# A decoder layer in split float32 on one core: the mixers' weights split once and reread, value differences in place of a masked subtraction, 512-column queries, early norm sums, and Down's sums on VectorE

## Chip, cores and metric

One core of a Trainium2 chip runs the whole program. The metric is the device time of one execution in microseconds (us), as a median of several runs. The engines are named as the profile names them: PE (TensorE matmuls), PEld (its weight loads), DVE (VectorE), ACT (ScalarE), POOL (GpSimd) and SP (SyncE, which issues most DMAs).

## What is computed

```python
h = rms_norm(x, attn_norm_g);  z = h @ w_in        # 2048 x 1024 by 1024 x 2304
q, k, v, gate_b, gate_c, xc = columns of z          # 8 query heads, 2 key/value heads of 64
q, k = rms_norm(q), rms_norm(k)
y_attn = softmax over 128 keys back, with a learned sink per head     # sliding window
y_conv = gate_b * short_conv(gate_c * xc, conv_w)   # 3 taps, causal
x = x + concat(rms_norm(y_attn), rms_norm(y_conv)) @ w_out
x = x + square(relu(rms_norm(x) @ w_up)) @ w_down   # 1024 -> 4096 -> 1024
```

All inputs and the output are float32; there is one layer and one batch of 2048 positions.

## The kernel before

**Split products.** Each float32 operand of a product is kept as two parts, high and low: the high part is a rounded copy, made by ACT, and the low part is what is left, made by DVE. `mm3` then issues three matmuls (high by high, high by low, low by high), lines L217 to L219.

**Mixers.** The positions go in four chunks of 512 (`CH`), each of four tiles of 128. Per chunk, `project_qkv` computes queries, keys and values in three pieces of 256 columns; `conv_pair` runs twice over the three convolution gates; `out_projection` runs for the convolution half (`part` 1) and, in the next chunk, for the attention half (`part` 0). Each of the 13 weight blocks of a chunk (2048 float32 per partition, 1 MB) is loaded by `load` into one of two `raw` buffers and split by `split` into one of two `whl` buffers: four ACT copies (L193, or L197 with a gain) and four DVE subtractions (L195, L198). The next chunk loads and splits them again.

**Order of the work.** Attention runs block by block (`scores`, then `values`), and between its steps `fill` lets the PE take a number of steps from a generator with the rest of the chunk's matmuls. The numbers are in the table `FILL`; `PRIO` moves groups of instructions earlier or later in the order of ACT, DVE, POOL and SP. Each engine, SP's queue included, works strictly in its own order.

**Attention's second half.** A block of queries sees two blocks of keys with a triangular mask. In `values`, `probabilities` transposes the probabilities into PSUM, makes the high part on ACT (L477) and the low part on DVE (L478); POOL copies out the triangle of the block's own keys (L482, `part`), and DVE subtracts it from the whole (L491), so that `full` holds only the previous block's keys. Then four matmuls (L511) multiply the two with the previous and the own values.

**MLP.** Up and Down are products of 2x2 blocks that are done with seven products in place of eight, so sums of blocks are needed. Down's products come in the order 5, 3, 1, 2, 6, 7, 4; each has 16 groups, and its weights and operands are loaded two steps ahead by `ready_down`, in SP's order. After product 6, `down_out` makes four sums of 128 x 2048 (L819, `tt`, on POOL) for each of two row halves, and stores a finished block with SP (L1183).

Of the kernel before, what the change touches and what calls it, by code (L numbers as in the profile page):

```python
# [7 lines left out]
F32 = mybir.dt.float32  # L8
# [82 lines left out]
def hymba_layer(  # L91
# [50 lines left out]


# [19 lines left out]
    nc.scalar.activation(warm, mhalf[:, :1], AF.Square)  # L163
    mean = const.tile([P, 1], F32, name="mean")
# [14 lines left out]
    def load(src_list, name):  # L179

        raw = pool.tile([P, 2048], F32, tag="raw", name=f"raw_{name}", bufs=2)
        for dst, src in src_list(raw):
            nc.sync.dma_start(dst, src)
        return raw

    def split(raw, name, gains=(None,) * 4, sub=(nc.vector,)):

        hl = pool.tile([P, 2, 2048], F32R, tag="whl", name=f"w_{name}", bufs=2)
        with ahead(7):
            for i, g in enumerate(gains):  # L190
                r = slice(i * 512, (i + 1) * 512)
                if g is None:
                    nc.scalar.copy(hl[:, 0, r], raw[:, r])  # L193
                    eng = sub[i % len(sub)]
                    eng.tensor_tensor(hl[:, 1, r], raw[:, r], hl[:, 0, r].bitcast(F32), op=ALU.subtract)  # L195
                else:
                    nc.scalar.activation(hl[:, 0, r], raw[:, r], AF.Copy, scale=g)  # L197
                    nc.vector.scalar_tensor_tensor(  # L198
                        hl[:, 1, r], raw[:, r], g, hl[:, 0, r].bitcast(F32), op0=ALU.mult, op1=ALU.subtract
                    )  # L200
        return hl

    def weights(src_list, name, **kw_):
        return split(load(src_list, name), name, **kw_)
# [16 lines left out]
    def norm_stats(xt, name):  # L221
# [3 lines left out]
        rs = small.tile([P, 1], F32, tag="rs", name=f"rs_{name}", bufs=2)  # L225
# [87 lines left out]
    z0 = [row("z", f"z0_{t}", NT) for t in range(NT)]  # L313
    raw0 = pool.tile([P, 2048], F32, tag="raw", name="raw_qkv0_0", bufs=2)
    hl0 = pool.tile([P, 2, 2048], F32R, tag="whl", name="w_qkv0_0", bufs=2)
# [3 lines left out]
    def split0(i, eng):  # L319
        r = slice(i * 512, (i + 1) * 512)  # L320
        nc.scalar.copy(hl0[:, 0, r], raw0[:, r])
        eng.tensor_tensor(hl0[:, 1, r], raw0[:, r], hl0[:, 0, r].bitcast(F32), op=ALU.subtract)
# [33 lines left out]
    with tc.tile_pool(name="mix_small", bufs=1) as mix_small, tc.tile_pool(name="mix", bufs=1) as mix:  # L356
# [4 lines left out]
        vz = mix.tile([P, 2, KVH, 2, 2, DH], F32R, name="vz")  # L361
        def project_qkv(c, h, z):

            z += z0 if not c else [row("z", f"z{c}_{t}", NT) for t in range(NT)]
            for pc in range(3):
                hl = hl0 if c + pc == 0 else weights(cols256(wi, pc * 256), f"qkv{c}_{pc}")
                w4 = hl.rearrange("p s (k c) -> p s k c", k=KD)
                for t in range(NT):
                    ps = bank("mm", f"pz{c}_{pc}_{t}")[:, :256]
                    hk = lambda s, k, t=t: h[s][:, k, t * P : (t + 1) * P]  # L370
                    for i in range(3 if c + pc + t == 0 else 0):
                        for k in range(KD):
                            nc.tensor.matmul(
                                ps, hk(i // 2, k), w4[:, i % 2, k, :], start=i + k == 0, stop=i + k == KD + 1
                            )
                    for k in range(KD if c + pc + t else 0):
                        mm3(ps, lambda s, k=k: hk(s, k), lambda s, k=k: w4[:, s, k, :], k == 0, k == KD - 1)
                        if k % 2 and k < KD - 1:
                            yield
                    nc.scalar.copy(z[t][:, pc * 256 : (pc + 1) * 256], ps)  # L380
# [82 lines left out]
        def values(b, zt, sc, n_fill, fill):  # L463
# [3 lines left out]
            def probabilities(kv):  # L467
# [10 lines left out]
                nc.vector.tensor_tensor(p0[:, 1, :], pt, p0[:, 0, :].bitcast(F32), op=ALU.subtract)  # L478
                if b:
                    for i in range(2):  # L480
# [10 lines left out]
                        nc.vector.tensor_tensor(full, full.bitcast(F32), part.bitcast(F32), op=ALU.subtract)  # L491
                    return [(1 - own, pp[0]), (own, pp[1])]
                return [(own, pp[0])]

            with ahead(4):
                for kv in range(KVH):
                    zv = zt[:, O_V + kv * DH : O_V + (kv + 1) * DH]
                    vh = vz[:, own, kv, :, kv, :]
                    nc.scalar.copy(vh, zv[:, None, :].to_broadcast([P, 2, DH]))
# [771 lines left out]
```

## Time and profile before

| what | value |
|---|---|
| time, median of 3 runs | 1991.6 us (1987.71 to 1996.96) |
| the profiled execution | 1995.26 us, with a span of 1993.6 us |
| PE busy | 1949.1 us, 98% of the span |
| DVE, ACT, POOL busy | 66%, 46%, 18% |
| mean granted PE clock | 0.988 of full |

The span runs from the first to the last instruction; the profiled execution's time is 1.7 us more. A matmul is pipelined, so the busy time of PE also covers the tail of each one, and the time from one matmul's start to the next says more of its pace. The stages lie in the span as follows: the first chunk's projection and mixers up to about 168 us, chunks 1 to 3 up to 749, Up to 1372, Down to 1990.

### The profile page before, as it was taken

The numbers are of one execution on the slowest core, as the hardware profiler recorded it, in microseconds if no ns is written. First come the engines' busy times: TensorE is split into PE (matmuls) and PEld (weight loads), VectorE is DVE, ScalarE is ACT, GpSimd is POOL, SyncE is SP. The second block draws the span as 40 slices with busy tenths as digits, with TensorE's granted clock in tenths as the row PEclk, the third lists the DMA queues.
The fourth block names the chain that finished last, engine by engine and source line by source line (L and its number), as shares of the span: only waits on it lengthen the run. The fifth ranks groups of instructions, "written<-read, shape, count | busy, mean of one in ns | idle before, by whom it ended". The sixth has DMA issues, their size and how long they took to land. (4 is left out here: it accounts for less than half of the span.)

```text
span 1993.6 us, 25599 instructions
## 1 busy us (share of the span) xinstructions
PE 1949.1 (98%) x9356; PEld 1630.0 (82%) x9356; DVE 1313.0 (66%) x1964; ACT 919.4 (46%) x1718; POOL 353.7 (18%) x455
## 2 busy tenths in 40 slices
PE   8999999999999999999999999999999999999989
PEld 7879887987988777888888888888888888888877
DVE  4787778678777878877778767666633334545551
ACT  4555455445546546555456555454432232222230
POOL 2231223304132420232201111111000000008000
PEclk9999999999999899999999999999999999999999
DMA  7214522352442379667666454437954447865651
GB/s 244 79 60 116 169 85 84 106 169 64 128 144 100 81 223 314 221 202 224 213 224 231 159 168 137 155 122 260 378 206 148 146 154 239 304 202 179 218 173 43
DMA packets 234190, 342.56 MB, mean 172 GB/s; under 512 B 17232, under 2 KB 148304, under 8 KB 234064
## 3 DMA queue, kind: packets, MB, share of 16 engines
q1 hardware_dynamic: 207120, 271.70, 42.5%
q0 software_dynamic: 13120, 44.05, 6.1%
q10 hardware_dynamic: 13824, 25.17, 3.4%
q8 instruction: 74, 1.21, 0.2%
q14 instruction: 52, 0.43, 0.1%
HBM read 242.31 MB, written 98.57 MB: 171 GB/s over the span
## 5 line engine op out<-in xcount | busy, mean ns | idle before, releaser
L1141 PE MATMUL u<-op_x,wop 128*128 128x512 f32 x2688 | 618.1, 391 | 2.0 <-DVE op_x L812 1.3
L1233 PE MATMUL d<-op_w,op_f 128*128 128x512 f32 x2688 | 612.5, 390 | 5.2 <-DVE d L1187 5.2
L1233 PEld LDWEIGHTS d<-op_w,op_f 128*128 128x128 f32 x2688 | 506.5, 188 | 110.8 <-issue 5.6
L1141 PEld LDWEIGHTS u<-op_x,wop 128*128 128x128 f32 x2688 | 505.2, 188 | 108.5 <-DVE op_x L812 1.6
L812 DVE TENSOR_TENSOR op_f<-op_f 128x1024 fp32r<-128x1024 f32 x112 | 144.4, 1293 | 251.6 <-ACT op_f L811 251.5
L811 ACT CAST op_f<-op_f 128x1024 fp32r<-128x1024 f32 x112 | 117.5, 1050 | 325.8 <-DMA op_f<-fop 324.5
L877 ACT CAST wop<-wu 128x512 fp32r<-128x512 f32 x160 | 98.9, 620 | 111.5 <-PE u L1141 105.1
L878 DVE TENSOR_TENSOR wop<-wu,wop 128x512 fp32r<-128x512 f32 x160 | 110.2, 690 | 41.2 <-ACT wop L877 25.8
L889 POOL DMA_DIRECT2D fop<-s x96 | 52.4, 546 | 427.2 <-DVE s L892 407.7
L895 DVE TENSOR_TENSOR u<-u,u 128x512 f32<-128x512 f32 x128 | 87.9, 687 | 25.1 <-PE u L1141 24.5
L812 DVE TENSOR_TENSOR op_w<-raw,op_w 128x1024 fp32r<-128x1024 f32 x56 | 72.6, 1297 | 37.2 <-ACT op_w L811 37.0
L811 ACT CAST op_w<-raw 128x1024 fp32r<-128x1024 f32 x56 | 58.9, 1052 | 63.1 <-PE d L1233 40.1
L218 PE MATMUL pz<-w_qkv,h_h 128*128 128x256 f32 x288 | 82.3, 286 | 0.0
L217 PE MATMUL pz<-w_qkv,h_h 128*128 128x256 f32 x288 | 82.1, 285 | 0.0
L219 PE MATMUL pz<-w_qkv,h_h 128*128 128x256 f32 x288 | 81.6, 284 | 0.0
L1097 POOL DMA_DIRECT2D wds<-raw x16 | 8.5, 534 | 344.4 <-DVE raw L1095 344.4
L452 ACT ACTIVATE sc_b<-sc_b,ngm_b 128x128 f32<-128x128 f32 x128 | 49.6, 390 | 28.7 <-DVE ngm_b L449 28.7
L482 POOL TENSOR_SCALAR_AFFINE_SELECT pp_b<-pp_b 128x512 fp32r<-128x512 f32 x60 | 48.2, 816 | 77.6 <-PE po_b L511 37.1
L198 DVE SCALAR_TENSOR_TENSOR w_wo<-raw_wo,g_y,w_wo 128x512 fp32r<-128x512 f32 x64 | 50.2, 798 | 12.9 <-ACT w_wo L197 12.9
L491 DVE TENSOR_TENSOR pp_b<-pp_b,pp_b 128x512 fp32r<-128x512 f32 x60 | 53.3, 921 | 6.1 <-POOL pp_b L482 6.1
L217 PE MATMUL pout<-w_wo,yt_c 128*128 128x512 f32 x128 | 55.2, 432 | 2.1 <-ACT yt_c L592 2.1
L877 ACT CAST wop<-wu_s 128x512 fp32r<-128x512 f32 x64 | 39.6, 620 | 37.9 <-PE u L1141 35.9
(225 smaller groups left out, 3425.1 us busy)
## 6 DMA issues: line engine op xcount, KB each, us to landing
op_f<-fop SPq DMA_DIRECT2D x112, 512.0 KB, 3.9
raw<-in_w_down_dram SPq DMA_DIRECT2D x72, 512.0 KB, 4.3
wu<-in_w_up_dram SPq DMA_DIRECT2D x128, 256.0 KB, 3.3
fop<-s POOLq DMA_DIRECT2D x96, 256.0 KB, 2.6
fop<-u ACTq DMA_DIRECT2D x64, 256.0 KB, 2.5
op_x<-xop SPq DMA_DIRECT2D x28, 512.0 KB, 6.4
raw_qkv<-in_w_in_dram SPq DMA_DIRECT2D x11, 1024.0 KB, 5.3
x<-in_x_dram SPq DMA_DIRECT2D x20, 512.0 KB, 6.7
```

The costliest lines, as they stand in the source:

```text
L217: nc.tensor.matmul(ps, st(0), mv(0), start=first, stop=False)
L218: nc.tensor.matmul(ps, st(0), mv(1), start=False, stop=False)
L219: nc.tensor.matmul(ps, st(1), mv(0), start=False, stop=last)
L491: nc.vector.tensor_tensor(full, full.bitcast(F32), part.bitcast(F32), op=ALU.subtract)
L811: nc.scalar.copy(op[:, 0], raw)
L812: nc.vector.tensor_tensor(op[:, 1], raw, op[:, 0].bitcast(F32), op=ALU.subtract)
L877: nc.scalar.copy(hi, blk)
L878: nc.vector.tensor_tensor(lo, blk, hi.bitcast(F32), op=ALU.subtract)
L889: eng.dma_start(fop_dram[tb][ORDER_DOWN.index(i)][n // 2][:, n % 2], b)
L895: nc.vector.tensor_tensor(dst, ps, b, op=ALU.add)
L1141: nc.tensor.matmul(pt, wops[i][:, a, k, :], xops[tb, p][k // 2][:, b, k % 2, :], start=p not in GOES_ON and k + j == 0, stop=k + j == NB + ...
L1233: nc.tensor.matmul(ps[tb][j], fs[tb][:, a, k, j * P : (j + 1) * P], w[:, b, k, :], start=first and p not in GOES_ON and k + n == 0, stop=l ...
```

## The change

1. **Weights split once.** In chunk 0 the two parts of each block are stored to DRAM (`keep`); chunks 1 to 3 load the parts (2 x 1 MB) straight into the buffers that the matmuls read. The buffers are four tiles `w`, and from the second chunk on every third block takes the two `raw` tiles. The attention half of `w_out` is first used in chunk 1, so its split and store fall there.
2. **Queries in 512 columns.** In chunks 1 to 3 `project_qkv` computes all queries in one piece with two weight blocks, then keys and values in 256 columns.
3. **Value differences.** With V the values, full x V_before + part x (V_own - V_before) replaces the subtraction on DVE: `full` stays unmasked, POOL makes the difference of the values (128 x 128), ACT and DVE split it into `vd`.
4. **Order.** In the first column half of the convolution's `out_projection`, tiles 0 to 2 do their first three products, then their last ones, then comes tile 3; the convolution's norm (`pc`) comes after 8 of these steps instead of 3 (`PC`); the last block's attention norm after 5 steps of the next chunk instead of 2 (`REST`). `PRIO` and `FILL` have new numbers.
5. **Norm sums.** The MLP's sums of squares are made right after the residual sum of each tile, into `rs_x1`, instead of when the tile is read again.
6. **Down.** Product 5 is added to a residual block on DVE (before: copied by ACT). The sums after product 6 run on DVE in pieces of 128 x 512, two pieces of each half per step; one sum of each half is gone. Stores before product 4 go by POOL's queue.

```diff
-DOWN_BUFS = {"u": 4, "x1": 5}
+DOWN_BUFS = {"u": 2, "x1": 7}
-PC = (0, 2)
+PC = (2, 1)
+REST = 5
+LATER = 250
...
-    (40, 0, 60, -10, 10, 0, 30, 10, 0, 30, 0, 0),
+    (220, 0, 60, -50, 40, 0, 270, 10, 50, 240, 0, 0),
...
-    ((20, 16), (9, 16, 11, 8, 1), (9, 8, 11, 8, 2), (11, 11, 15, 6, 5), (9, 15, 11, 5, 3)),
+    ((25, 18), (9, 16, 11, 8, 1), (9, 8, 11, 3, 2), (11, 9, 15, 6, 5), (9, 15, 11, 5, 3)),
...
+    def high_low(c, name):
+        n_pieces[0] += 1
+        tag, bufs = ("raw", 2) if c and n_pieces[0] % 3 == 0 else ("w", 4)
+        return [pool.tile([P, 2048], F32R, tag=tag, name=f"{name}_{i}", bufs=bufs) for i in range(2)]
+    def keep(hl, name):
+        parts_dram[name] = [dram.tile([P, 2048], F32, name=f"{name}_{i}") for i in range(2)]
+        with tc.high_priority(offset=-LATER):
+            for d, t in zip(parts_dram[name], hl):
+                nc.sync.dma_start(d, t.bitcast(F32))
+    def weights(src_list, c, name, gains=(None,) * 4):
+        if c:
+            hl = high_low(c, f"w_{name}{c}")
+            for d, t in zip(parts_dram[name], hl):
+                nc.sync.dma_start(t.bitcast(F32), d)
+            return hl
...
+                n = 256 if pc else AW
                 for t in range(NT):
...
+                    for k in range(KD):
+                        mm3(ps, lambda s, k=k: hk(s, k), lambda s, k=k: wk(s, k), k == 0, k == KD - 1)
...
-                        nc.vector.tensor_tensor(full, full.bitcast(F32), part.bitcast(F32), op=ALU.subtract)
-                    return [(1 - own, pp[0]), (own, pp[1])]
+                    return [(vz[:, 1 - own], pp[0]), (vd, pp[1])]
...
+                if b:
+                    nc.gpsimd.tensor_tensor(v_diff, zt[:, O_V:O_B], v_before, op=ALU.subtract)
...
+                if half and not dh:
+                    order = sorted(order, key=lambda x: (x[0] == NT - 1, x[1] == NCT - 1))
...
                             eng.dma_start(x1_dram[r : r + P, :], x1[t])
+                            norm_stats(x1[t], f"m{c}_{t}", rs_x1[:, c * NT + t : c * NT + t + 1])
...
-                    if i == 2:
+                    if i == REST:
                         attn_rstd(b, sqa, ra[:, NT - 1 : NT])
...
         elif p == 5:
-            v["u4"] = block("u", f"d4_{tb}")
-            for j in range(NB):
-                nc.scalar.copy(v["u4"][:, j], ps[j])
+            add(v["u4"], ps, v["u4"])
...
         elif p == 6:
             add(v["u2"], ps, v["u2"])
-            plus(v["12"], v["u2"])
-            for j in range(NB):
-                put(1, 2, v["12"], j)
-            plus(v["u4"], v["u2"])
-            v["22"] = residual(2, 2)
-            plus(v["u4"], v["22"])
             v["21"] = residual(2, 1)
-            plus(v["u2"], v["21"])
+            def sums():
+                yield from plus(v["u4"], v["u2"])
+                yield from plus(v["12"], v["u2"])
+                for j in range(NB):
+                    put(1, 2, v["12"], j)
+                yield from plus(v["u2"], v["21"])
+            later.append(sums())
```

Three places show how the order moves. The first is PE's order before, where chunk 1's convolution ends (`po_b` are the products with the values of block 5, `pout` is the output projection, `ptq_b` the next block's transposed queries):

```order
L511 MATMUL po_b_0_3177<-pp_b_0_0_3125,vz 128x512 [waits DVE_49,Activation_49]
L511 MATMUL po_b_0_3177<-pp_b_0_0_3125,vz 128x512 [waits DVE_49]
L511 MATMUL po_b_0_3177<-pp_b_0_1_3126,vz 128x512 [waits Pool_49] x2
...
L511 MATMUL po_b_1_3225<-pp_b_1_0_3138,vz 128x512 [waits DVE_49,Activation_49]
L408 MATMUL ptq_b_3242<-ident,z_3_1809 128x128 [waits PE_49]
...
L511 MATMUL po_b_1_3225<-pp_b_1_0_3138,vz 128x512 [waits DVE_49]
L511 MATMUL po_b_1_3225<-pp_b_1_1_3139,vz 128x512 [waits Pool_49] x2
```

The same products in the changed program (`pt_a` are the next chunk's transposes):

```order
L588 MATMUL po_b_0_3147<-pp_b_0_0_3085,vz 128x512 [waits Activation_49]
L588 MATMUL po_b_0_3147<-pp_b_0_0_3085,vz 128x512 [waits DVE_49]
L273 MATMUL pt_a_0_0_3194<-ident,xt_a_0_3121 128x128 [waits DVE_49]
...
L588 MATMUL po_b_0_3147<-pp_b_0_1_3086,vd 128x512 [waits Pool_49] x2
...
L588 MATMUL po_b_1_3158<-pp_b_1_0_3096,vz 128x512
L475 MATMUL ptq_b_3175<-ident,z_3_1871 128x128 x4
...
L588 MATMUL po_b_1_3158<-pp_b_1_0_3096,vz 128x512
L588 MATMUL po_b_1_3158<-pp_b_1_1_3097,vd 128x512 [waits Pool_49] x2
```

The second head's first product waited for DVE and ACT; now it carries no wait of its own, and only the triangular part waits for POOL.

SP's queue in Down before, after product 6 (`out_dram<-x` stores the finished block, `op_f` loads an operand of product 7, `x_1_21` a residual block):

```order
L1086 DMA raw_0_21_15691<-in_w_down_dram 128x2x512 [waits DMAHW6_49,DMAHW0_49,DVE_49]
L1183 DMA out_dram<-x_0_12_13190 128x512 [waits DMAHW1_49,Pool_49]
L1183 DMA out_dram<-x_0_12_13190 128x512
...
L1178 DMA x_1_21_15296<-x_dram 128x4x512 [waits DMAHW5_49,Pool_49]
L1183 DMA out_dram<-x_1_12_13221 128x512 [waits Pool_49]
...
L810 DMA op_f_0_4_15443<-fop_5_4_128 128x1024 [waits DMAHW2_49,PE_49]
L810 DMA op_f_1_4_15447<-fop_5_4_184 128x1024 [waits DMAHW3_49,PE_49]
```

SP's queue near the same place in the changed program:

```order
L1167 DMA raw_4_22_14920<-in_w_down_dram 128x2x512 [waits DMAHW6_49,DMAHW0_49,DVE_49]
L896 DMA op_f_0_0_14644<-fop_5_0_124 128x1024 [waits DMAHW1_49,PE_49]
L1167 DMA raw_4_12_14922<-in_w_down_dram 128x2x512 [waits DVE_49]
L896 DMA op_f_1_0_14648<-fop_5_0_180 128x1024 [waits DMAHW3_49,PE_49]
L1167 DMA raw_5_22_14988<-in_w_down_dram 128x2x512 [waits DMAHW4_49,DMAHW2_49,DVE_49]
```

The stores that waited for POOL are no longer between the loads.

## Rows read from the trace of the kernel before

**Rows 1.** Busy time of PE, its share of the span and its instructions (first part of the page).

```profile
PE 1949.1 (98%) x9356; PEld 1630.0 (82%) x9356; DVE 1313.0 (66%) x1964; ACT 919.4 (46%) x1718; POOL 353.7 (18%) x455
```

**Rows 2.** The trace in stretches: start and end in us, length, then busy time (and instructions) of PE, PEld, DVE, ACT and POOL, mean granted PE clock, busy share of the DMA engines, GB/s moved. Chunk 0, chunk 1, Down.

```profile
18.00:168.00 150.00, 146.72 (x841) 127.08 (x841) 110.85 (x206) 83.16 (x219) 34.56 (x43) 0.98 0.35 112
168.00:347.00 179.00, 173.07 (x961) 148.18 (x960) 139.95 (x261) 95.30 (x238) 47.90 (x59) 0.99 0.35 110
1372.00:1990.00 618.00, 612.30 (x2689) 506.26 (x2687) 270.84 (x237) 178.10 (x180) 51.31 (x28) 0.99 0.59 204
```

**Rows 3.** What PE waited for in the whole span: what waited, for what, us in total, times, longest.

```profile
PE pt_a L244 <- DVE x L232: 9.1, 2, 7.9
PE po_b L511 <- ACT y_c L597: 5.4, 2, 3.2
PE d L1233 <- DVE d L1187: 5.2, 1, 5.2
PE po_b L511 <- DVE pp_b L491: 4.6, 5, 1.5
PE pout L219 <- POOL yt_c L593: 3.0, 2, 1.6
PE pout L217 <- ACT yt_c L592: 2.1, 2, 1.4
PE pt_m L258 <- DVE xt_m L232: 1.7, 3, 1.2
PE pa_b L532 <- DVE o_b L527: 1.6, 2, 0.9
PE u L1141 <- DVE op_x L812: 1.3, 1, 1.3
PE pa_b L532 <- ACT w_wo L197: 1.1, 2, 0.5
PE pout L217 <- DVE x L632: 0.9, 1, 0.9
```

**Rows 4.** The seven stretches after the start in which the granted clock was at the lower level; columns as in rows 2.

```profile
133.60:140.40 6.80, 6.48 (x21) 4.88 (x20) 3.97 (x5) 2.27 (x4) 3.92 (x5) 0.50 0.16 53
314.50:317.90 3.40, 3.40 (x11) 2.83 (x12) 3.37 (x6) 1.33 (x4) 1.53 (x1) 0.50 0.00 0
495.40:502.20 6.80, 6.80 (x22) 5.65 (x21) 6.55 (x14) 4.79 (x12) 1.37 (x2) 0.50 0.02 7
679.70:689.90 10.20, 9.29 (x32) 8.04 (x33) 5.79 (x9) 3.52 (x6) 5.67 (x6) 0.50 0.00 0
717.30:724.10 6.80, 5.86 (x19) 4.38 (x20) 5.22 (x7) 2.94 (x5) 1.00 (x3) 0.50 0.61 181
751.40:758.20 6.80, 6.26 (x15) 4.59 (x15) 3.19 (x5) 2.10 (x4) 0.36 (x6) 0.50 1.11 365
1898.30:1905.10 6.80, 5.57 (x13) 4.44 (x14) 6.16 (x9) 1.04 (x1) 0.00 (x0) 0.50 0.95 323
```

**Rows 5.** Four matmuls in order of time (start us, us, engine, line, operation): two of 256 columns, 33 matmuls apart, and two of 512 columns, 30 apart.

```profile
38.08 0.28 PE L219 MATMUL pz<-w_qkv,h_a 128*128 128x256 f32 x1
42.04 0.28 PE L219 MATMUL pz<-w_qkv,h_a 128*128 128x256 f32 x1
...
741.26 0.40 PE L217 MATMUL pout<-w_wo,at_b 128*128 128x512 f32 x1
748.10 0.39 PE L217 MATMUL pout<-w_wo,at_b 128*128 128x512 f32 x1
```

**Rows 6.** The chain behind the longest wait of chunk 1, and the chain from the last convolution product of chunk 0 to its sum of squares; columns as in rows 5, with the idle time before and its releaser in brackets.

```profile
312.55 2.35 DVE L491 TENSOR_TENSOR pp_b<-pp_b,pp_b 128x512 fp32r<-128x512 f32 x2
314.45 0.73 PE L511 MATMUL po_b<-pp_b,vz 128*128 128x512 f32 x1 [3.16 <-ACT y_c L597]
...
128.66 0.68 DVE L589 TENSOR_TENSOR y_c<-pb_c,y_c 128x512 f32<-128x512 f32 x1
133.92 1.27 POOL L598 TENSOR_TENSOR ssc<-ssc,y_c 128x512 f32<-128x512 f32 x1
```

**Rows 7.** Down after product 6: POOL's first sum, SP's first blocked stores, POOL's sums' end, SP's next load of an operand.

```profile
1803.13 5.63 POOL L819 TENSOR_TENSOR x<-x,d 128x2048 f32<-128x2048 f32 x1 [83.89 <-issue]
1808.79 1.81 SPq L1183 DMA_DIRECT2D out_dram<-x  x4
1829.99 1.79 SPq L1183 DMA_DIRECT2D out_dram<-x  x4
1831.89 1.76 SPq L810 DMA_DIRECT2D op_f<-fop  x3
```

**Rows 8.** Groups of instructions over the span: line, engine, operation, out<-in, shapes, count, busy us, mean ns, idle before.

```profile
L198 DVE SCALAR_TENSOR_TENSOR w_wo<-raw_wo,g_y,w_wo 128x512 fp32r<-128x512 f32 x64 | 50.2, 798 | 12.9 <-ACT w_wo L197 12.9
L195 DVE TENSOR_TENSOR w_wc_c<-raw_wc_c,w_wc_c 128x512 fp32r<-128x512 f32 x32 | 21.7, 716 | 9.1 <-ACT w_wc_c L193 9.0
L491 DVE TENSOR_TENSOR pp_b<-pp_b,pp_b 128x512 fp32r<-128x512 f32 x60 | 53.3, 921 | 6.1 <-POOL pp_b L482 6.1
```

**Rows 9.** DMA loads of 1 MB: count, KB each, median us from issue to landing; and one stretch of Down with the DMA engines full (columns as in rows 2).

```profile
raw_wc_c<-in_w_in_dram SPq DMA_DIRECT2D x8, 1024.0 KB, 5.5
x<-x_dram SPq DMA_DIRECT2D x8, 1024.0 KB, 7.7
...
1390.00:1395.00 5.00, 5.00 (x24) 4.14 (x23) 2.34 (x3) 0.93 (x2) 0.00 (x0) 1.00 1.03 415
```

More of the change, by code (lines that the diff above doesn't have):

```diff
@@ L141, in row, with zrow @@
         return pool.tile([P, D], dt, tag=tag, name=name, bufs=bufs)
+    def zrow(name):
+        return pool.tile([P, O_B], F32, tag="z", name=name, bufs=NT)
     small.tile([P, 16], F32, name="pad")
@@ L177, in ahead, with raw_part @@
         return tc.high_priority(offset=offset) if offset else nullcontext()
-    def load(src_list, name):
-        raw = pool.tile([P, 2048], F32, tag="raw", name=f"raw_{name}", bufs=2)
+    parts_dram = {}
+    n_pieces = [0]
+    def raw_part(name):
+        return pool.tile([P, 2048], F32, tag="raw", name=name, bufs=2)
+    def high_low(c, name):
[13 more added lines that the diff above has]
+            return hl
+        raw = raw_part(f"raw_{name}")
         for dst, src in src_list(raw):
             nc.sync.dma_start(dst, src)
-        return raw
-    def split(raw, name, gains=(None,) * 4, sub=(nc.vector,)):
-        hl = pool.tile([P, 2, 2048], F32R, tag="whl", name=f"w_{name}", bufs=2)
+        hl = high_low(c, f"w_{name}")
         with ahead(7):
@@ L224, in norm_stats @@
         nc.scalar.activation(junk, xt, AF.Square, scale=D**-0.5, accum_out=ss)
-        rs = small.tile([P, 1], F32, tag="rs", name=f"rs_{name}", bufs=2)
+        if rs is None:
+            rs = small.tile([P, 1], F32, tag="rs", name=f"rs_{name}", bufs=2)
         rsqrt(rs, ss)
@@ L312, in hymba_layer @@
     load_x0 = lambda t: nc.sync.dma_start(x0[t], xf[t * P : (t + 1) * P, :])
-    z0 = [row("z", f"z0_{t}", NT) for t in range(NT)]
-    raw0 = pool.tile([P, 2048], F32, tag="raw", name="raw_qkv0_0", bufs=2)
-    hl0 = pool.tile([P, 2, 2048], F32R, tag="whl", name="w_qkv0_0", bufs=2)
+    z0 = [zrow(f"z0_{t}") for t in range(NT)]
+    raw0 = raw_part("raw_qkv0")
+    hl0 = high_low(0, "w_qkv0")
     h = parts(pool, "h", "a0")
@@ L368, in project_qkv @@
                 for t in range(NT):
-                    ps = bank("mm", f"pz{c}_{pc}_{t}")[:, :256]
+                    ps = bank("mm", f"pz{c}_{pc}_{t}")[:, :n]
                     hk = lambda s, k, t=t: h[s][:, k, t * P : (t + 1) * P]
[L371 to L375, printed above, removed]
@@ L376, in project_qkv @@
-                    for k in range(KD if c + pc + t else 0):
-                        mm3(ps, lambda s, k=k: hk(s, k), lambda s, k=k: w4[:, s, k, :], k == 0, k == KD - 1)
-                        if k % 2 and k < KD - 1:
+                    for k in range(KD):
+                        mm3(ps, lambda s, k=k: hk(s, k), lambda s, k=k: wk(s, k), k == 0, k == KD - 1)
+                        if (k % 2 or not pc) and k < KD - 1:
                             yield
-                    nc.scalar.copy(z[t][:, pc * 256 : (pc + 1) * 256], ps)
+                    nc.scalar.copy(z[t][:, pc * AW : pc * AW + n], ps)
@@ L599, in conv_pair, with out_projection @@
                 yield
-        def out_projection(c, part, ys, rs, x1):
+        def out_projection(c, half, ys, rs, x1):
             for dh in range(2):
@@ L607, in src @@
                     r3 = raw.rearrange("p (i c) -> p i c", i=NCT)
-                    if part:
+                    if half:
                         return [(r3, wo[AW:, cs].rearrange("(i p) c -> p i c", p=P))]
@@ L634, in out_projection @@
                         )
-                        if dh and not part:
+                        if dh and not half:
                             r = (c * NT + t) * P
@@ L1222, in hymba_layer @@
     ps, vs = {}, {tb: {} for tb in range(NTB)}
+    later = []
     for i, (p, g) in enumerate(steps):
         ready_down(i + LEAD_DOWN)
+        for x in later:
+            next(x, None)
         first, last = not g, g == NCG // 2 - 1
@@ L1240, in hymba_layer @@
                         )
+            if i == NCG // 4:
+                down_out(tb, p, None, vs[tb])
             if last:
```

144 lines of the change are left out of this document (97 added, 47 removed), and 12 rows, old and new, of tables (FILL, PRIO).

## The prediction

> **What bounds the kernel now.** I read the first part of the page first: PE is busy for 1949.1 of 1993.6 us [rows 1], so the kernel is a stream of matmuls, and a change can gain only in three ways: cheaper matmuls, fewer stops of PE, and less time at the lower clock. So three views follow. The timeline gives the pace: 33 matmuls of 256 columns start in 42.04 - 38.08 = 3.96 us, 120 ns each, and 30 of 512 columns in 6.84 us, 228 ns each [rows 5]. The waits of PE give the stops: the eleven largest add up to 36.0 us, of which 9.1 belong to the start, which does not change [rows 3]. The rest falls into few kinds: 10.0 us before the products with the values (5.4 + 4.6), 5.1 before the output projection for the convolution's last results (3.0 + 2.1), 2.7 before the attention's norm (1.6 + 1.1), 5.2 once in Down, 3.9 around the MLP's start (1.7 + 1.3 + 0.9). The stretches give the clock: seven times after the start the granted clock is 0.5, that is 1.2 of 2.4 GHz, for 47.6 us together [rows 4]. PE is busy for 43.7 of them, and at the full clock that work would take half, so they cost up to 21.8 us. The first four follow waits of the first two kinds (PE had stood still for 1.5 to 3.2 us shortly before), the last follows the wait in Down; the fifth and sixth lie at the change from mixers to MLP.
>
> What makes PE wait in the mixers is a late chain on the other engines. DVE is busy for 140 of 179 us in chunk 1 [rows 2], and every chain there crosses it several times behind other work.
>
> **Queries in 512 columns.** Three chunks x 4 tiles x 8 slabs x 3 products = 288 matmuls of 512 columns replace 576 of 256. Each pair takes 2 x 120 = 240 ns, its successor 228 [rows 5]. Gain: 288 x 12 ns = **3.5 us**, all on the path, since PE is the path.
>
> The Trainium skill, "TensorE: Matmul & The Clock Gate", section "Back-to-back issue gap", gives 262 cycles for 256 columns and 518 for 512; by that a pair would gain some 2.5 ns and the whole step 0.7 us, and the sum below would end 2.8 us higher. The trace does not show that pace at either width, and the sum goes by the trace.
>
> **Down.** POOL's first sum starts at 1803.1 and the second half's is done at 1830; SP, with the stores of that block ahead of its loads, stands from 1808.8 to 1831.9 [rows 7]. So the next operands come late, the splits behind them as well, and DVE reaches the sums of product 7, which PE needs before it may go on in the same banks, only when PE has stood still for 5.2 us [rows 3]. Behind it the clock falls for 6.8 us with 5.57 us of PE work, half of that lost: 2.8 [rows 4]. The change takes the sums from POOL, and the stores from SP's queue, so SP has nothing to wait for. DVE takes 2 x (4 + 12) = 32 pieces instead; at the 0.92 us of its costliest subtraction of that size [rows 8] they are 29 us in a stage where it works 271 of 618 [rows 2]. Product 5's add stands before product 3's use of the same banks: 4 x 0.92 = 3.7 us against the other half's 24 matmuls, 5.5 us, so I cost it at nothing; uncovered it would be 3.7 us, twice at most. Gain: **8.0 us** (0 to 8.0).
>
> **Weights split once.** Per chunk 9 x 4 pieces at 0.716 and 4 x 4 at 0.798 us leave DVE [rows 8]: 38.5 us, and as many instructions leave ACT. The masked subtraction, 60 x 0.921 us, takes another 13 us of each chunk [rows 8]. DVE's load in chunk 1 falls from 140 to about 88 of 179 us; the new splits of value differences give at most 8 x 0.72 = 6 back. None of this counts by itself; it counts where PE waits, below. In its place stand DMAs. Each later chunk loads 13 blocks of 1.05 MB more, 13.6 MB or 76 GB/s on top of 110 [rows 2]; the stores, 11 blocks of 2.1 MB in the 150 us of chunk 0, add 154 GB/s to 112 there. Down shows 415 GB/s [rows 9], so the engines have room. A single block has two loads: 5.5 us for the first and 2.5 more for the second at that rate [rows 9], 8.0 us. The shortest cover I find in the changed order is one block's matmuls (2 groups x 24 x 0.228 = 10.9 us) between the freeing of a buffer and the use of the next content, once in chunk 1; elsewhere 15 us and more. Cost: nothing. With the slower row, 7.7 us per MB [rows 9], the cover would be gone; that is a rival below.
>
> **Value differences.** In the longest wait of chunk 1 DVE subtracts twice, from 312.55 to 314.90, once POOL has cut its triangles, and PE goes on at 314.45 after 3.16 us of idling [rows 6]. The subtraction goes, the first two of four products need no triangle at all, and in the new order the second head's first product has no wait of its own. What is late next is POOL's triangle for the last two products, with other matmuls ahead of it. POOL's new difference of 128 x 128 values needs only the projection, which is done long before. Of 10.0 us [rows 3] I take **9** (5 to 10).
>
> **Order of the output projection.** From the first step on the last convolution product to the sum of squares 6.5 us pass (128.66 to 135.19) [rows 6]. Before, PE had one tile's first three steps of other work (9 x 0.228 = 2.1 us) until it needed the last result; now it has nine (6.2 us), and the norm comes after 8 steps (5.5 us). Of 5.1 us I take **4** (2 to 5.1). A new wait is possible: three tiles now hold all three banks until the norm factor is there. The trace before does not show it. It lies between nothing and the wait that it replaces, 1.6 us in each of four chunks [rows 3]; I set **4 us lost** in all for this and any other new stop (0 to 6.4).
>
> **Attention norm later, norm sums early.** The last block's norm gets three more steps, 2.0 us, against waits of at most 0.9 [rows 3]: of 2.7 I take **2**. The norm sums leave the chain before the MLP's transposes: of 1.7 + 0.9 I take **1.5**. The sums themselves cost ACT and POOL as much as before. The 1.3 at Up's start stays.
>
> **Clock.** The four stretches behind the first two kinds of wait hold 26.0 us of PE work [rows 4], 13.0 lost. When most of these waits go, I take **10** (4 to 13). The two at the MLP's start (12.1, 6.1 lost) I leave.
>
> **Sum.** -3.5 - 8.0 - 9 - 4 - 2 - 1.5 - 10 + 4 = -34.0 us. The profiled execution took 1995.3 us, so 1961.3; it lies 3.7 us above the median of 1991.6, and against that the forecast is 1957.6, rounded to **1958 us**.
>
> **Rivals.**
> - *Nothing much in the mixers* (0.14). The waits move: POOL's triangle and the norm factor become what ends last, and the clock falls as before. For it: POOL's chain stays, and the three banks are held longer. Against it: the new order has products without waits where PE waited. Left are 3.5 + 8.0 us: 1980, between 1972 and 1985.
> - *All of it* (0.12). Every stop named goes, and the clock stays up: 3.5 + 8.0 + 10.0 + 5.1 + 2.7 + 2.6 + 1.3 + 13.0 + 6.1 = 52.3, so 1939 us. For it: DVE's load falls by a third. Against it: Up's start is not touched, and chains of five steps remain.
> - *Weights late, slower* (0.05). The matmuls of chunks 1 to 3 now wait for loads directly. A chunk has 179 / 13 = 13.8 us per block; if two loads of 1 MB take longer, the DMA sets the pace. At 7.7 us each [rows 9] it is 15.4, so 1.6 us x 39 blocks = 62 us lost, and 1958 + 62 = 2020 us. It decides from 13.8 us per block, and costs the whole gain near 14.7. Against it: the DMA engines are busy for 0.35 of chunk 1 [rows 2], and weight blocks land in 5.5 us.
>
> The forecast itself holds 0.69, from 1944 to 1972.
>
> **How the numbers follow.** A measurement of this kernel can tell about 0.5% (10 us) from no change, so faster means below 1981.6. The forecast and the second rival are faster, and half of the first: 0.69 + 0.12 + 0.07 = 0.88. The other half of the first is no change, 0.07; the third is slower, 0.05. The range leaves out the ends of the rivals: 1941 to 1979 holds the forecast, half of "all of it" and a third of "nothing much", 0.80.
>
> **What would show it.** In the changed profile: `pz` with 512 columns at 228 ns from start to start; no wait of `d` for DVE and full clock from Up to the end; waits of `po_b` together under 2 us, and none on DVE; fewer than four stretches at half clock in the mixers; DVE near 50% busy in chunks 1 to 3; and hardly any wait of PE for a DMA. The forecast is wrong if PE waits for `w_` loads by more than some us, if `po_b` or the third `pout` tile stands for POOL or the norm factor, or if the clock falls in every chunk as before.

## Result, and the profile after

The changed kernel takes 1981.66 us (median of six runs, 1975.79 to 1984.14), the kernel before 1992.98 (1987.71 to 1998.38): a ratio of 0.9937, 95% interval 0.9912 to 0.9961. The forecast was 1958 us, 1941 to 1979. So it is faster, by a third of what was forecast. The profiled execution took 1980.8 us, with a span of 1978.8.

First the page of the changed kernel, busy time and the two groups that hold two thirds of it (columns as in [rows 1] and [rows 8]):

```profile
PE 1945.1 (98%) x9068; PEld 1608.4 (81%) x9068; DVE 1189.2 (60%) x1810; ACT 837.2 (42%) x1572; POOL 317.2 (16%) x492
...
L1222 PE MATMUL u<-op_x,wop 128*128 128x512 f32 x2688 | 634.0, 397 | 4.6 <-ACT wop L963 4.5
L1328 PE MATMUL d<-op_w,op_f 128*128 128x512 f32 x2688 | 609.6, 389 | 0.0
```

The same two groups of the kernel before:

```profile
L1141 PE MATMUL u<-op_x,wop 128*128 128x512 f32 x2688 | 618.1, 391 | 2.0 <-DVE op_x L812 1.3 <-DVE wop L878 0.5 <-ACT wop L877 0.2
L1233 PE MATMUL d<-op_w,op_f 128*128 128x512 f32 x2688 | 612.5, 390 | 5.2 <-DVE d L1187 5.2
```

Down lost its wait. But Up, with the same 2688 matmuls in the same order on PE, is busy 15.9 us longer. A stretch of Up in which nothing waits shows it best: how many matmuls start in 200 us (columns as in [rows 2]), before,

```profile
1100.00:1300.00 200.00, 200.00 (x884) 165.62 (x883) 140.61 (x216) 103.84 (x172) 23.75 (x44) 1.00 0.48 155
```

and after:

```profile
1100.00:1300.00 200.00, 200.00 (x859) 160.91 (x858) 137.20 (x212) 99.81 (x166) 25.75 (x48) 1.00 0.46 157
```

That is 226 ns a matmul before and 233 after, at the full clock in both. DVE, ACT and the DMA engines are busy for no more of these 200 us than before, POOL for 2.0 us more. By the starts of the records nearly every interval of Up was 226 or 227 ns; now they alternate between 229 and 238.

The largest waits of PE, which answer to [rows 3]:

```profile
PE pt_a L273 <- DVE x L261: 9.2, 2, 8.1
PE ptq_b L475 <- DVE z L464: 6.8, 3, 2.9
PE u L1222 <- ACT wop L963: 4.5, 1, 4.5
PE pt_a L273 <- DVE ms_c L784: 4.3, 2, 2.2
PE pt_a L273 <- DVE ms_b L611: 2.5, 1, 2.5
PE po_b L588 <- POOL pp_b L551: 0.8, 2, 0.5
PE pt_m L287 <- ACT xm L288: 0.6, 1, 0.6
```

Of the old kinds, 0.8 us of `po_b` and 0.6 of `pt_m` are left. The other rows below the start's are new: the next chunk's query transposes wait for their norm, the transposes of the next input (`pt_a`) for DVE to copy a norm's sums out of the one bank of PSUM (the memory that takes PE's sums) that they share, and Up's first product for its weights.

The stretches at the lower clock that answer to [rows 4], four in the mixers and one at Up's start:

```profile
130.28:133.70 3.42, 3.42 (x11) 2.65 (x10) 3.42 (x7) 2.34 (x4) 2.66 (x3) 0.50 0.97 325
201.96:205.38 3.42, 3.42 (x16) 3.23 (x16) 2.84 (x5) 1.99 (x6) 1.94 (x2) 0.50 0.46 101
318.02:324.84 6.82, 5.99 (x26) 5.84 (x27) 4.57 (x14) 2.95 (x8) 3.61 (x5) 0.50 0.00 1
379.46:382.87 3.41, 3.41 (x18) 3.31 (x17) 3.06 (x7) 2.36 (x6) 2.23 (x2) 0.50 0.01 2
727.62:734.44 6.82, 5.73 (x13) 4.06 (x14) 4.47 (x6) 2.81 (x5) 0.30 (x6) 0.50 1.12 360
```

Each begins 1.5 to 3.7 us after PE came to one of the new stops; two more stops, at 494 and 552 us, have no such stretch.

**Where the time went.** I take the interval from each matmul's start to the next, less its pace (227, 120, 70 and 28 ns for 512, 256, 128 and 1 columns). What exceeds it at half clock is "clock", a single excess over 0.4 us a "stop", the rest "small". Mixers run from 18 us to the first `u` (a product of Up), Up from there to the first `d` (of Down); lengths and parts in us:

| stage | before: length | pace | clock | stops | small | after: length | pace | clock | stops | small |
|---|---|---|---|---|---|---|---|---|---|---|
| mixers | 731.2 | 658.3 | 12.2 | 25.9 | 34.7 | 710.6 | 654.7 | 7.2 | 21.5 | 27.1 |
| Up | 617.1 | 609.2 | 2.8 | 2.4 | 2.7 | 631.2 | 609.2 | 2.5 | 0.0 | 19.5 |
| Down | 627.2 | 615.4 | 2.8 | 5.1 | -0.5 | 618.9 | 615.4 | 0.0 | 0.0 | -0.4 |

So the mixers gained 20.6 us, Down 8.3, and Up gave back 14.1. (What the parts leave of Down's length, some 4 us, lies behind the last matmul.)

### The profile page after: what moved, and what is told of

It is laid out like the page before. It is cut to its first block, busy times and chain, and to the rows that moved or that the text cites. A ratio compares the mean times of both kernels' runs of the same rounds, so it can differ in the third digit from the quotient of the medians.

```text
span 1978.8 us, 24773 instructions
## 1 busy us (share of the span) xinstructions
PE 1945.1 (98%) x9068; PEld 1608.4 (81%) x9068; DVE 1189.2 (60%) x1810; ACT 837.2 (42%) x1572; POOL 317.2 (16%) x492
## 4 chain that ended last, share of the span: by engine, by line
PE 93%; DVE 3%; POOL 1%; ACT 1%; DMA 1%; issue 1%; SPq 0%; DVEq 0%; POOLq 0%; ACTq 0%
PE u L1222 32%; PE d L1328 31%; PE pout L245 3%; PE pout L247 3%; PE pout L246 3%; PE pz L246 2%; PE pz L245 2%; PE pz L247 2%; PE psc_b L502 1%; PE pc_c L246 1%; PE pc_c L245 1%; PE pc_c L247 1%; PE px_c L245 1%; PE px_c L247 1%; PE px_c L246 1%; PE pb_c L247 1%
## 5 line engine op out<-in xcount | busy, mean ns | idle before, releaser
L1222 PE MATMUL u<-op_x,wop 128*128 128x512 f32 x2688 | 634.0, 397 | 4.6 <-ACT wop L963 4.5
L898 DVE TENSOR_TENSOR op_f<-op_f 128x1024 fp32r<-128x1024 f32 x112 | 136.7, 1224 | 237.2 <-ACT op_f L897 237.1
L898 DVE TENSOR_TENSOR op_w<-raw,op_w 128x1024 fp32r<-128x1024 f32 x56 | 68.4, 1223 | 34.1 <-ACT op_w L897 33.9
L551 POOL TENSOR_SCALAR_AFFINE_SELECT pp_b<-pp_b 128x512 fp32r<-128x512 f32 x60 | 42.7, 725 | 111.6 <-ACT pp_b L544 73.1
L987 ACT ACTIVATE u<-u 128x512 f32<-128x512 f32 x64 | 40.5, 633 | 33.9 <-DVE u L981 30.9
L245 PE MATMUL pout<-w_wo,yt_c 128*128 128x512 f32 x128 | 52.8, 412 | 0.0
L247 PE MATMUL pout<-w_wo,yt_c 128*128 128x512 f32 x128 | 52.5, 410 | 0.0
L246 PE MATMUL pout<-w_wo,yt_c 128*128 128x512 f32 x128 | 51.9, 406 | 0.0
L245 PE MATMUL pout<-w_wo,at_b 128*128 128x512 f32 x128 | 50.2, 392 | 0.0
L247 PE MATMUL pout<-w_wo,at_b 128*128 128x512 f32 x128 | 50.0, 391 | 0.0
```

The costliest lines, as they stand in the source:

```text
L245: nc.tensor.matmul(ps, st(0), mv(0), start=first, stop=False)
L246: nc.tensor.matmul(ps, st(0), mv(1), start=False, stop=False)
L247: nc.tensor.matmul(ps, st(1), mv(0), start=False, stop=last)
L898: nc.vector.tensor_tensor(op[:, 1], raw, op[:, 0].bitcast(F32), op=ALU.subtract)
L1222: nc.tensor.matmul(pt, wops[i][:, a, k, :], xops[tb, p][k // 2][:, b, k % 2, :], start=p not in GOES_ON and k + j == 0, stop=k + j == NB + ...
```

## Experiments: why Up became slower

Theory A: the new tile of norm factors `rs_x1` is 128 bytes per partition, and everything allocated behind it on the left side of SBUF, the memory from which the engines read, moved by that. Up's weights `wop` (the operand that PEld loads) stood at 128 modulo 256 bytes, and now stand at 0 (one of their buffers: from address 84352 to 84480); the moving operand `op_x`, allocated from the right end, stayed at 128 (114560). Rival B: other work of the changed program is in Up's way. The edit, with n floats of 4 bytes:

```diff
     pool = up_ctx.enter_context(tc.tile_pool(name="mlp_up", bufs=1, reuse_waits="tile"))
+    pool.tile([P, n], F32, name="up_pad")
```

n = 96 in the changed kernel. 

> The changed kernel with 384 unused bytes per partition ahead of Up's left-hand tiles, so that the weight tiles of Up (wop) start at 384 modulo 512 bytes, as in the kernel before; the order of all instructions is that of the changed kernel. Theory A (the 128 bytes of the new tile of norm factors moved wop to another place, and that place costs some 6 ns per matmul of Up): Up's matmuls start 227 ns apart again, its stage takes some 621 us instead of 637, and the whole 1966 us. Theory B (Up is slower because other work of the changed program, DVE, ACT or DMA, gets in its way): Up's matmuls stay at 229 and 238 ns, and the whole at 1981.

n = 32 in the kernel before. 

> The kernel before with 128 unused bytes per partition ahead of Up's left-hand tiles, so that wop starts at 0 modulo 512 bytes, as in the changed kernel, and nothing else changed. Theory A (the place of the tiles): Up's matmuls take 229 and 238 ns from start to start, the stage is some 15 us longer, the whole 2007 us. Theory B (other work of the changed program): no change, 1992.

n = 32 in the changed kernel. 

> The changed kernel with 128 unused bytes ahead of Up's left-hand tiles: wop at 128 modulo 512 (128 modulo 256, as in the kernel before). If the place modulo 256 decides, Up runs at 227 ns and the whole takes 1966 us; if it is modulo 512, or a single bad place, this tells which: 1966 if only 0 is bad, 1981 if all but 384 are. Theory B: 1981.

n = 64 in the changed kernel. 

> The changed kernel with 256 unused bytes ahead of Up's left-hand tiles: wop at 256 modulo 512 (0 modulo 256, as in the changed kernel). If the place modulo 256 decides, Up stays at 229 and 238 ns and the whole at 1981 us; if only 0 modulo 512 is bad, 1966. Theory B: 1981.

Then the other operand is moved in place of the first:

```diff
     fill = ops.tile([P, 24], F32, tag="fill", name="fill")
+    ops.tile([P, 32], F32, name="ops_pad")
```

> The changed kernel with the right-hand tiles of the MLP moved by 128 bytes, so that Up's moving operand (op_x) starts at 0 modulo 256 bytes as its weights (wop) do, and both of Down's operands too; the left-hand tiles stay where the change put them. If what costs is that the two operands of a matmul stand at different places modulo 256 bytes: Up runs at 227 ns and the whole takes 1966 us. If wop's own place costs: Up stays at 229 and 238 ns, 1981 us. If 0 modulo 256 costs for any operand: Down slows as well, by some 16 us, 1997 us.

Last, n = 16 in the changed kernel. 

> The changed kernel with 64 unused bytes ahead of Up's left-hand tiles: wop at 64 modulo 256 bytes, op_x at 128. If any difference modulo 256 bytes costs as much: Up at 229 and 238 ns, 1981 us. If only a difference of 128 costs: 1966 us. If the cost grows with the distance: between, some 1973 us.

Measured ("small" is Up's, as in the table above; a ratio is to the kernel before as it ran beside that kernel):

| kernel | wop, op_x modulo 256 | time (us) | ratio to before (95%) | small (us) |
|---|---|---|---|---|
| before | 128, 128 | 1992.98 | 1 | 2.7 |
| changed | 0, 128 | 1981.66 | 0.9937 (0.9912 to 0.9961) | 19.5 |
| e1 | 128, 128 | 1965.98 | 0.9867 (0.9846 to 0.9888) | 2.8 |
| e2 (before, moved) | 0, 128 | 2006.46 | 1.0071 (1.0047 to 1.0095) | 18.7 |
| e3 | 128, 128 | 1963.98 | 0.9858 (0.9836 to 0.9880) | 2.7 |
| e4 | 0, 128 | 1980.51 | 0.9942 (0.9926 to 0.9959) | 19.4 |
| e8 | 0, 0 | 1965.90 | 0.9869 (0.9843 to 0.9895) | 2.9 |
| e15 | 64, 128 | 1971.54 | 0.9890 (0.9875 to 0.9905) | 8.0 |

The same 200 us of Up in e2, the kernel before with nothing but unused bytes,

```profile
1100.00:1300.00 200.00, 200.00 (x862) 162.17 (x861) 136.12 (x210) 100.46 (x166) 23.85 (x44) 1.00 0.45 153
```

in e3,

```profile
1100.00:1300.00 200.00, 200.00 (x884) 165.58 (x884) 140.13 (x216) 102.00 (x169) 23.84 (x44) 1.00 0.47 153
```

in e8,

```profile
1100.00:1300.00 200.00, 200.00 (x884) 165.70 (x883) 139.35 (x215) 102.36 (x170) 24.73 (x46) 1.00 0.45 153
```

and in e15:

```profile
1100.00:1300.00 200.00, 200.00 (x876) 164.12 (x875) 139.65 (x215) 101.56 (x169) 24.29 (x45) 1.00 0.48 155
```

Theory A holds and B is out: unused bytes alone slow the kernel before and mend the changed one. It is no bad place as such, since with both sides at 0 (e8) Up is as quick as with both at 128, and Down, whose operands both moved, as well; what costs is that the two sides differ modulo 256 bytes. At a difference of 64 it costs a third. That the period is 256 bytes and not more is seen from e1 and e3, 256 bytes apart and both quick, and from the changed kernel and e4, 256 bytes apart and both slow. All left-hand tiles moved together, so that it is the matmul's two operands that count is argued, not shown by itself. Two facts speak for it: in the built program Up's matmuls are the only instructions of that stage that touch tiles of both sides, but for four that prepare Down; and in the mixers, where the change moved both operands of every 512-column product from 128 to 0, the most frequent intervals are 226 and 227 ns before and after.

**e3 is the base of what follows**, but for e14: the change as it was meant, without the side effect. It takes 1964 us, and its mixers have 7.1 us of clock, 23.1 of stops and 27.3 of small delays.

## Experiments: the forecast's terms, undone one by one

The value differences, out of e3:

```diff
+                        nc.vector.tensor_tensor(full, full.bitcast(F32), part.bitcast(F32), op=ALU.subtract)
-                    return [(vz[:, 1 - own], pp[0]), (vd, pp[1])]
+                    return [(vz[:, 1 - own], pp[0]), (vz[:, own], pp[1])]
...
```

> The changed kernel with 128 unused bytes ahead of Up's tiles (1964.0 us), with the value differences undone: DVE subtracts the triangle from the probabilities again, and the products use the previous and the own values. Theory A (the forecast's step: the subtraction is what po_b waits for): waits of po_b come back, 9 us (5 to 10), and with the clock 1973 to 1976 us. Rival (with the weights' splits gone DVE comes to the subtraction at once, and the new order covers the rest): under 3 us of new stops, 1964 to 1967 us.

1975.87 us, ratio 0.9913 (0.9896 to 0.9929), with 33.8 us of stops and this row among the waits of PE:

```profile
PE po_b L583 <- DVE pp_b L560: 7.8, 10, 2.0
```

Theory A: the stops rose from 23.1 us by 10.7, most of it in this row.

The weights split in every chunk, out of e3 (no loads of parts, no stores; the two query blocks loaded raw and split):

```diff
-        if c:
-            hl = high_low(c, f"w_{name}{c}")
-            for d, t in zip(parts_dram[name], hl):
-                nc.sync.dma_start(t.bitcast(F32), d)
-            return hl
...
```

> The changed kernel with 128 unused bytes ahead of Up's tiles, but with each weight block loaded raw and split in every chunk, as in the kernel before, and no parts stored (four buffers w, two raw; the queries stay in 512 columns, their two blocks split after loading). Theory A (DVE's load sets how late its chains are): DVE is busy again for some 140 of 179 us in chunk 1, stops and short delays of PE in the mixers rise from 23 + 27 to some 35 + 35 us, 1984 us in all. Rival (DVE's load does not count, the order does): 1964 to 1968 us.

1977.31 us, 0.9920 (0.9905 to 0.9934). Chunk 1 in the stretches (columns as in [rows 2]), e3:

```profile
161.00:340.00 179.00, 173.94 (x871) 147.20 (x870) 104.42 (x209) 79.76 (x220) 51.32 (x73) 0.97 0.56 197
```

e11:

```profile
161.00:340.00 179.00, 168.24 (x845) 140.78 (x844) 126.34 (x245) 100.28 (x258) 52.56 (x73) 0.98 0.35 109
```

The rival is out: to split again costs 13 us, 9.8 of them stops (32.9 in all). The small delays hardly moved (28.8), against theory A. The added load is not DVE's alone: ACT splits as well, 100 of 179 us in place of 80, and this run does not part the two.

The queries in pieces of 256 columns, out of e3:

```diff
-            if not c:
+            if True:
                 for pc in range(3):
...
```

> The changed kernel with 128 unused bytes ahead of Up's tiles, with queries, keys and values in three pieces of 256 columns again, from the stored parts. By the pace of the trace (2 x 120 against 228 ns, 288 times) it is 3.5 us longer, 1967.5 us; by the page's gap 0.7 us longer, 1964.7 us. Rival (the order shifts with the other pieces, and stops weigh more than the pace): off by more than 3 us in either direction.

1974.93 us, 0.9909 (0.9894 to 0.9924). The pace of the mixers is 658.4 us against 654.8: 3.6, as the trace of the kernel before had it. The rest of the 11 us is the rival's: 5.1 us more stops, 2.2 more clock, with order numbers that were set for the other pieces. One of these stops is a wait for a load of parts, which no other run here shows: 1.8 us for `w_wc`.

Down's edits alone, in the kernel before (all code from the pool of Down on, and `DOWN_BUFS`).

> The kernel before with the change in Down alone. Theory A (the forecast's step): Down has no wait and full clock, 8.3 us less as in the changed kernel's trace, 1985 us. Rival (the wait in Down went because the changed mixers and Up brought other loads' timing): the wait stays, 1993 us.

1984.19 us, 0.9956 (0.9942 to 0.9970), 8.8 us less; Down has no stop and no stretch at half clock. Theory A.

## Experiments: the new stops

In e5 the query transposes come later on PE:

```diff
-    (220, 0, 60, -50, 40, 0, 270, 10, 50, 240, 0, 0),
-    (200, 0, 220, -50, 40, 0, 260, 0, 30, 240, 0, 10),
-    (200, 20, 180, -10, 0, 0, 40, 20, 0, 0, 0, 0),
+    (40, 0, 60, -50, 40, 0, 270, 10, 50, 240, 0, 0),
+    (40, 0, 220, -50, 40, 0, 260, 0, 30, 240, 0, 10),
+    (40, 20, 180, -10, 0, 0, 40, 20, 0, 0, 0, 0),
```

> The changed kernel with 128 unused bytes ahead of Up's tiles (1964.0 us, its stops of PE in the mixers 23.1 us), and with the first number of PRIO back at 40 in chunks 1 to 3 (220, 200, 200 in the change), so that the transposes of a chunk's first queries come some 80 to 110 instructions later on PE, behind steps of the output projection. Theory A (the three stops between chunks, 3.03 + 2.12 + 2.11 us, come from transposes that were moved too far ahead of the norm of the queries): they go, 1957 us. Rival (the chain of the first block is then late elsewhere: scores, probabilities or the products with the values stop PE instead): 1964 us or more.

1969.03 us, 0.9886 (0.9866 to 0.9905): the rival. `ptq_b` no longer waits, but the norm of the last block does:

```profile
PE pa_b L609 <- DVE o_b L604: 5.4, 2, 2.7
PE pa_b L609 <- ACT w_wo L227: 1.8, 1, 1.8
```

So e9 moves that norm too (`REST` from 5 to 9, on top of e5).

> The kernel of e5 (128 unused bytes ahead of Up's tiles, first number of PRIO at 40 in chunks 1 to 3), and with the last block's attention norm after 9 steps of the next chunk instead of 5, which puts 4 x 3 x 0.228 = 2.7 us more of matmuls ahead of pa_b. Theory A (in e5 the stops between chunks only moved from ptq_b to pa_b, 2.01 + 2.86 + 2.85 us, and both can be covered by the output projection's steps): all three go, 1957 us. Rival (the chain of the first block or the norm factor for the last tile is now late): 1964 us or more.

1967.95 us, 0.9873 (0.9857 to 0.9890): again the rival. In chunk 1 the stops fell from 3.03 to 1.44 us, but in chunks 2 and 3 the output projection now stands for DVE to add a finished product to the residual (L716), which frees its bank:

```profile
PE pout L245 <- DVE x L716: 8.2, 3, 4.0
```

The chain there, from the timeline of e9 (columns as in [rows 6]):

```profile
380.68 1.99 POOL L178 TENSOR_TENSOR rq_b<-ssq_b,mhalf 128x10 f32<-128x10 f32 x1
...
382.70 0.89 DVE L462 TENSOR_TENSOR z<-z,rq_b 128x640 f32<-128x640 f32 x1 [2.21 <-POOL rq_b L178]
383.51 0.28 DVE L604 TENSOR_TENSOR o_b<-o_b 128x128 f32<-128x128 f32 x1
...
387.76 1.07 DVE L462 TENSOR_TENSOR z<-z,rq_b 128x640 f32<-128x640 f32 x1 [2.31 <-POOL rq_b L178]
388.86 0.75 DVE L716 SCALAR_TENSOR_TENSOR x<-pout,ra,x 128x512 f32<-128x512 f32 x1
...
389.67 0.51 PE L245 MATMUL pout<-w_wo,at_b 128*128 128x512 f32 x1 [3.94 <-DVE x L716]
```

DVE stands 2.21 us for the queries' norm factor of one tile, which POOL takes 1.99 us to make, and the last block's sum of squares (L604) is queued behind it, for which PE stood in e5. It stands 2.31 us for the factor of the next tile, and the add (L716) is queued behind that, for which PE stands in e9. That one of the two chains is late whichever step PE takes first is argued from these rows; a quicker factor, or another order on DVE, was not tried.

In e6 the convolution's norm gets a bank of its own:

```diff
-                        pc = bank("tr", f"pc{c}")
+                        pc = bank("at", f"pc{c}")
```

> The changed kernel with 128 unused bytes ahead of Up's tiles, and with the convolution's norm (pc) in one of the four PSUM banks of the attention instead of the single bank of the transposes. Theory A (the stops of pt_a in chunks 1 and 2, 2.11 + 2.37 us, come from the one bank, held until DVE has copied pc): they go, some 1959.5 us; the stop at 127 us, which waits for the attention's norm pa_b in the same bank, stays. Rival (DVE is late in any case, and an attention bank is now missed): the stops move to scores or products with the values, 1964 us or more.

1968.93 us, 0.9885 (0.9865 to 0.9905), 28.6 us of stops: the rival. `pt_a` now waits for DVE's half of its own copy:

```profile
PE pt_a L273 <- DVE h_h L278: 6.0, 3, 2.8
```

At Up's start I tried three things. e7 makes the last chunk's norm sums late, when Up reads the tiles (`if c + 1 < NCHUNK:` ahead of `norm_stats`, and the old sums in `prepare_rest`).

> The changed kernel with 128 unused bytes ahead of Up's tiles, and with the norm sums of the last chunk's four tiles made where the kernel before made them, when Up reads the tiles again; the other chunks keep the early sums. Theory A (at Up's start ACT has the last tile's sum of squares, which waits for PE's last product, ahead of the splits of Up's first operands; so PE stands 5.9 us in place of some 1.5): the stop falls to some 2 us, 1960 us in all. Rival (the loads of Up's first operands set the start): PE stands as long, 1964 us.

e13 issues the first weight loads ahead of the operands':

```diff
+    with tc.high_priority(offset=150):
+        while wanted and wanted[0][0] <= PRE - LEAD:
+            _, n, x = wanted.pop(0)
+            wts.setdefault(n, Weights(n, later=False)).piece(*x)
     ready_x(0)
```

> The changed kernel with 128 unused bytes ahead of Up's tiles (1964.0 us), with the loads of Up's first six weight pieces issued ahead of the loads of its first operands (they stood behind them, and those wait for the last stores of the operands). Theory A (at Up's start PE stands 5.9 us for the weight pieces, which share the queue with operands that come late): the weights start some 3 us earlier, the stop falls to some 3 us, 1961 us. Rival (the operands themselves, or the rate of the DMA engines, set the start): no change or a loss, 1964 us or more.

e17 is e7 with the first weight pieces elsewhere than under the mixers' last weight block:

```diff
+    for i in range(6):
+        nc.gpsimd.memset(piece("w", f"w_skip{i}")[:, :1], 0.0)
```

> The kernel of e7 (128 unused bytes ahead of Up's tiles, the last chunk's norm sums made late), with six weight buffers of Up passed over, so that the first weight pieces no longer go where the mixers' last weight block lies. Theory A (two waits end together at Up's start: ACT's queue behind the last sums, and the loads behind PE's last product; each hid the other): the stop of 5.9 us falls to 2 us or less, 1960 us in all. Rival (the loads are limited by their rate, or the operands come late): the stop stays at 4 us or more, 1964 us.

e7: 1963.62 us, 0.9857 (0.9833 to 0.9880), stop 5.4 us. e13: 1968.62, 0.9876 (0.9861 to 0.9891), stop 11.6. e17: 1965.05, 0.9860 (0.9843 to 0.9876), stop 4.6. Theory A fell three times. In e13 the weight loads stood in SP's queue until PE's last product, since they overwrite its weights, and the operands behind them:

```profile
714.13 12.92 SPq L941 DMA_DIRECT2D wu<-in_w_up_dram  x6
...
727.14 1.74 SPq L897 DMA_DIRECT2D op_x<-xop  x2
...
SPq L941 <- PE pout L247: 8.8, 1, 8.8
```

(The last row is from SP's waits, with columns as in [rows 3].) With that mended, in e17, the DMA engines are full (share 1.04, 388 GB/s) while PE stands:

```profile
721.00:726.00 5.00, 2.58 (x12) 1.81 (x10) 2.54 (x3) 1.44 (x2) 1.17 (x3) 1.00 1.04 388
```

The stop is 4.4 to 5.9 us in kernels that leave this place alone (e8, e3), so e7 and e17 gained nothing that can be told there. In e17 some 3 MB of loads begin when the operands' last stores are done, from 716.6 us on. That their rate is the cause is argued from this row; fewer bytes at that place were not tried.

e16 is e13 with chunk 1's part of e5 and e9, e18 is e17 with it:

```diff
-    (220, 0, 60, -50, 40, 0, 270, 10, 50, 240, 0, 0),
+    (40, 0, 60, -50, 40, 0, 270, 10, 50, 240, 0, 0),
...
-                    if i == REST:
+                    if i == (REST if c else 9):
```

> The kernel of e13 with two numbers more: the first number of PRIO at 40 in chunk 1, and the last block's norm of chunk 0 after 9 steps of chunk 1 instead of 5. In e9 this left 1.44 us of stops at that place in place of 3.03, while in chunks 2 and 3 it made 4 us out of 2. Theory A (the places are independent): 1.6 us less than e13, some 1959 us. Rival (what is taken here comes back later in the chunk): as e13.

> The kernel of e17 with the two numbers of e16 (first number of PRIO at 40 in chunk 1, the last block's norm of chunk 0 after 9 steps of chunk 1). Theory A: 1.6 us less than e17, some 1958 us, which is what the forecast gave for the change itself. Rival (the stops move): as e17, or 1964 us.

e16: 1966.49 us, 0.9861 (0.9843 to 0.9879), 2.7 us of stops less than e13. e18: 1960.35 us (1958.07 to 1964.81), 0.9842 (0.9823 to 0.9860): 19.2 us of stops. In both the stops ahead of chunk 1 fell by some 1.6 us, and those ahead of chunks 2 and 3 stayed at 2.1 us each: theory A. The 4.7 us between e17 and e18 are more than that; in the two traces, up to Up's start, e18 has 3.4 us at half clock and e17 17.1, which theory A did not name and which may be chance. e18 is faster than both kernels, though its interval overlaps that of e3.

## Why the prediction was wrong, step by step

**The step that failed** is what the sum says of Up: that only "the 1.3 at Up's start stays", and so that a stage with the same matmuls in the same order keeps its pace. Up's pace is a term that the sum puts at nothing without giving a reason. It lost 14.1 us. The change has a new constant tile, which I read as norm sums made early and not as 128 bytes that move Up's weights against the operand they meet. With the place put back the change takes 1964 or 1966 us (e3, e1), inside the range and the forecast's own 1944 to 1972. That it then comes so near to 1958 is in part luck: in the changed kernel's trace the new stops and the clock came out worse than forecast by 12.8 and 5.0 us, and the old waits, and the small delays that the sum left out, better by 2.5 and 7.6.

- *Queries*, 3.5: the pace fell by 3.6. Matmuls of `pz` with 512 columns, 9 apart, start in 2.03 us, 226 ns each (228 in the forecast). By the Trainium skill ("TensorE: Matmul & The Clock Gate", section "Back-to-back issue gap", the table of the isolated gap) the step would have given 0.7 us, with which these rows do not agree:

```profile
184.28 0.39 PE L245 MATMUL pz<-w_q,h_h 128*128 128x512 f32 x1
...
186.31 0.39 PE L245 MATMUL pz<-w_q,h_h 128*128 128x512 f32 x1
```

- *Down*, 8.0: 8.3, and 8.8 alone (e14). Right.
- *The old waits in the mixers*, 9 + 4 + 2 + 1.5 = 16.5: of 10.0 + 5.1 + 2.7 + 2.6 us [rows 3], 1.4 are left, so 19.0 went. Right in kind. For the products with the values e10 shows the reason given, the subtraction. For the attention's norm e11 and e12 bring back a wait of 4.6 us, so it hangs on the load and on the order. For the convolution's last results the reason is argued: none of their waits comes back in e11, and no run puts the old order of the output projection back.
- *New stops*, an allowance of 4 (0 to 6.4): 6.8 + 4.3 + 2.5, and 3.2 more at Up's start, 16.8 us. This is the second term that was mis-sized. I looked for them at the third bank of `pout`, where none is; they stand where the order had moved a step towards a chain (the query transposes to 220 steps ahead, `pc` right ahead of transposes in its bank) and where PE came to Up while its loads were under way.
- *Clock*, 10 (4 to 13): 5.0 in the mixers. By the intervals the five stretches there cost 12.2 us before, where half of PE's busy time in them [rows 4] gives 15.9. The old stretches went, but the new stops are followed by others; "fewer than four" was wrong, it is four.
- *Not in the sum*: small delays, 34.7 to 27.1. Undoing the value differences gives 2.4 of that back, the splits 1.5, the queries nothing; the rest stays open.
- *DVE in chunk 1*: 104 of 179 us, not 88. Of the 16 us, 6.2 are the eight pieces of `w_out`'s attention half that are still split in this chunk, as is said of the change; I had taken them away too. 3.0 are the splits of the value differences, for which I had named up to 6; the rest I can't place.
- *Weights late*: in the changed kernel PE waited for no load of parts.

The rival "nothing much in the mixers" names nearly the measured time, 1980, and is wrong: the mixers gained 20.6 us.

## What to carry to other kernels

Before a forecast compare the addresses of matmul operands before and after, not only the order: a small constant tile can cost more than a stage's tuning gains (here 14.1 us in Up against 8.3 in Down), and it does so where the diff shows nothing. When stops go, ask of each step that moved forward which chain it now meets; here stops that were moved on PE came back at the next step of the same chain (e5, e9). And read a gain from each stage's own time: the total hid 29 us of gain behind 14 of loss.

## What the runs showed of the hardware

Matmuls of 512 float32 columns start 226 ns apart when weights and moving operand stand at the same place modulo 256 bytes of a partition, whether both at 128 or both at 0; 228 at a difference of 64, and 233 at a difference of 128 (200 us divided by 884, 876 and 859 matmuls). At 128 the single intervals alternate between 229 and 238 in the changed kernel and lie between 228 and 241 in e2, with nearly the same mean (862 matmuls in 200 us). Over 2688 matmuls that was 5 and 17 us. The weight loads took 188 ns in both kernels. Other differences, and other widths, were not tried.
